# Re-pacing an expert-retrieval kernel: weight splits between VectorE and GpSimd, later one-hots, sums in DRAM

## The chip, the cores and the metric

The kernel runs on one core of a Trainium2 chip. The metric is the device time of one execution in microseconds (us), the median of several runs. The engines of a core run their own instruction queues in order: PE (TensorE, matmuls), DVE (VectorE), ACT (ScalarE), POOL (GpSimd) and SP (SyncE, which here only issues DMAs). POOL issues all indirect DMAs of this kernel, gathers and scatters.

## The reference, cut to what matters

Two layers. Each computes token mixers (attention of two kinds and a retention), an output projection, and then an expert retrieval ("PEER") that holds most of the work and all of the change:

```python
q = (h @ wq).reshape(t, 8, 2, 128)
s = einsum('thpd,hpnd->thpn', q, subkeys)          # two halves of a key, 128 values each
s_top, i_top = top_k(s, 16)                        # per half
cand = s_top[:, :, 0, :, None] + s_top[:, :, 1, None, :]
best, pos = top_k(cand, 16)                        # 16 experts of 128*128 per head, 8 heads
gate = softmax(best)
a = gelu(einsum('cd,chkd->chk', h, u[expert]))     # u, v: (16384, 1024) each
out = einsum('chk,chkd->cd', gate * a, v[expert])
```

Layer 0 has 768 tokens (6 tiles of 128: 0 to 3 latent, 4 and 5 context), layer 1 has 512 (tiles 0 to 3).

## The kernel before, in words

The retrieval is done densely: every 128x128 grid point (i, j) is an expert; for each column j the kernel multiplies 128 rows of u with all tokens of the "dense" tiles (four in layer 0, three in layer 1), takes Gelu, multiplies by a table of gates that is zero where a token did not pick the expert, and multiplies with 128 rows of v. Each layer runs four stages, which this document calls U0, U1 (upass, columns 0 to 63 and 64 to 127 of u) and V0, V1 (vpass, all 128 columns of v, for the first and the second group of tiles; groups are (2,3,4) and (5,0,1) in layer 0, (2,3) and (1,0) in layer 1). All matmuls are fp16 with each operand split into a high and a low half (three products). So every column of u and v is loaded (tile s), its high half made by ACT and its low half `hl` by DVE (L143 in U, L1114 in V); PE waits for both.

The gates come by three ways, spread through the stages as generators that a main loop advances a fixed number of steps per column (`tick`, with the rates `RATES`, `SRATES`, `RRATE`):

- Routing (`routing`, in U0): the query weights wq and the subkeys are split too (`wsplit`: ACT scales and casts, POOL subtracts, L153), PE makes scores (tiles rw, sc), DVE takes the top 16 (`top16`) and `pick` forms expert numbers and gates.
- Tiles 2 and 3: `Onehot.block` multiplies two one-hot matrices on PE, 8 tokens at a time; DVE makes the one-hots (L1194, L1198). There are 32 blocks for each half of the columns; those of half 0 end in a multiplication by DVE (L1213), those of half 1 in a copy by ACT (L1211). All 64 run in U1, one per column.
- The other tiles have a table in DRAM, 128x128x128 numbers. `Table.put` scatters one head's gates with 16 indirect DMAs (L1248, 128 numbers each); the first DMA of a head waits until the 16 of the head before it have landed. A token can pick an expert in several heads, so `pick` adds up equal experts before (128 small operations per tile, tile gjk, L919). V0 and V1 read the tables back. Tiles 4 and 5 (layer 0) and 1 (layer 1) are dense and put gates (table<-gs).
- Tiles 0 and 1 (layer 0) and 0 (layer 1) are "picked": `gather` fetches each of a token's 128 rows of u by an indirect DMA (L946, 128 rows of 4 KB into one of three buffers r), DVE multiplies it with h and sums (L952, two steps behind the gather), and the results are put (table<-a). h is held in PSUM (tile hp), so this operation has one SBUF input.

There are 384 gathers and 768 puts, all in POOL's one queue, in an order that the tile framework fixes when the kernel is built. DVE's queue is in order too: an L952 whose row has not landed holds up the `hl` behind it, and PE waits for that.

`queue_behind` orders a gather or put behind the last low-half split that was noted in `lo_ins`, in the planner's time only, with no semaphore.

Of the kernel before, what the change touches and what calls it, by code (L numbers as in the profile page):

```python
# [23 lines left out]
WS = 64.0  # L24
# [14 lines left out]
WLAG = 2  # L39
WADA = 7  # L40
# [6 lines left out]
class Hybrid:  # L47
# [89 lines left out]
    def split(self, hi, lo, src, scale=1.0, lo_eng=None):  # L137
        nc = self.nc
        nc.scalar.activation(hi, src, AF.Copy, scale=scale)  # L139
        if scale == 1.0:  # L140
            (lo_eng or nc.vector).tensor_tensor(lo, src, hi, op=OP.subtract)  # L141
        else:
            nc.vector.scalar_tensor_tensor(lo, src, scale, hi, op0=OP.mult, op1=OP.subtract)  # L143


    def wsplit(self, hi, lo, w, scale=WS, dve=False):
# [6 lines left out]
        self.lo_ins = nc.gpsimd.tensor_tensor(lo, w, hi, op=OP.subtract)  # L153
# [83 lines left out]
    def layer(self, l, last):  # L237
        with ExitStack() as es:
# [17 lines left out]
            self.vp = self.pool(es, "vs", 2)  # L256
            self.sp = self.pool(es, "sc", 2)
# [433 lines left out]
    def wout(self, l, es, last):  # L691
# [6 lines left out]
        def first(t):  # L698
# [13 lines left out]
            for c in (0, 512):  # L712
# [4 lines left out]
                v = pool.tile([128, 512], F32, name="wov")  # L717
# [41 lines left out]
    def routing(self, l, pool, ps, tiles, rp):  # L759
# [7 lines left out]
        def queries(b):  # L767
            sk = pool.tile([128, 128], F32, name="sk", bufs=3)
# [3 lines left out]
            self.wsplit(skh, skl, sk, SKS)  # L772
            ws = []
            for k in (0, 4):
                w = pool.tile([128, 4, 128], F32, name="wq", bufs=4)
# [3 lines left out]
                self.wsplit(wh, wl, w)  # L779
# [66 lines left out]
    def pick(self, l, t, sv, si, pool):  # L846
# [62 lines left out]
        if t in self.picked:  # L909
            ix = self.lp.tile([128, 16, 8], I32, name="ix", bufs=2)  # L910
# [58 lines left out]
    def peer(self, es, l, last, h2s):  # L969
        nc = self.nc  # L970
        self.hpp = self.pool(es, "hp", 1, space=PSUM)
# [8 lines left out]
        with ExitStack() as e:  # L980
# [8 lines left out]
            while self.unscored:  # L989
                self.step(self.rg, 1)  # L990
        h2s.close()
# [9 lines left out]
        with ExitStack() as e:  # L1001
            ps = self.pool(e, "ups", 4, space=PSUM)
            self.upass(l, 1, ps, "pa", PRATE[l], more)
        pws.close()
        self.accp = self.pool(es, "acc", 1, space=PSUM)
        for n, tiles in enumerate(self.groups):
            self.need(tiles)
            if n == 1 and not last:
                r = lambda: self.gp.tile([128, D], F32, name="r")
                vec = [self.srow(r(), 0, self.hpp.tile([128, D], F32, name="hp")), self.srow(r(), 1)]  # L1010
# [13 lines left out]
    def upass(self, l, half, ps, tag, rrate, more=None):  # L1024
# [5 lines left out]
        sb = {1: 4, 2: 2, 3: 2, 4: 1}[nd - first]  # L1030
        steps = iter(self.onehot) if half else iter(())
        def load(jj):
            u = self.vp.tile([128, KC, 128], F32, name="s4", bufs=3)
# [6 lines left out]
        for jj in range(64):  # L1040
# [5 lines left out]
            pa = ps.tile([128, 512], F32, name=tag)  # L1046
            for k in range(KC):
                self.mm3(pa[:, :nd * 128], uh[:, 0, k], uh[:, 1, k], hh[:, k], hl[:, k], k == 0, k == KC - 1)
# [10 lines left out]
            if jj >= 1:  # L1059
# [6 lines left out]
    def weights(self, tiles, j):  # L1066
# [3 lines left out]
        b = self.lp.tile([128, 2, n, 2, 128], F32, name="h2U" + "hl"[j // 2 % 2])  # L1070
        g, u = b[:, 0], b[:, 1].rearrange("p s j t -> p (s j t)").rearrange("p (j s t) -> p j s t", j=2, t=128)
# [7 lines left out]
        return g, u.rearrange("p j s t -> p s j t"), a  # L1079
# [20 lines left out]
    def vpass(self, l, tiles, n):  # L1100
# [4 lines left out]
        def load(j):  # L1105
            if j % 2 == 0:
                self.pr = self.weigh(tiles, j, *gs.pop(0))
# [229 lines left out]
```

## Time and profile before

| | |
|---|---|
| median of 3 runs | 5107.54 us (5106.78 to 5112.42) |
| profiled execution | 5100.45 us, of which the span of instructions is 5098.7 us |
| busy over the span | PE 82%, DVE 65%, ACT 38%, POOL 35% |
| granted TensorE clock, mean | 0.91 of full speed |

The profile is of one execution, and its own time is the one that a sum over its rows has to be made against. PE's 82% is a mean over stages. The stages of the retrieval, read from the first and the last matmul of each, begin as follows (us from the span's start): layer 0 U0 614, U1 1271, V0 1812, V1 2455 to 2980; layer 1 U0 3434, U1 3921, V0 4386, V1 4735 to 5085. What lies between is projection and attention.

### The profile page before, as it was taken

To read this page: it belongs to the slowest core of one execution; us is meant where nothing else is said; L and a number is where in the kernel's file an instruction comes from. 1 tells how busy PE (TensorE), PEld (TensorE's weight loads), DVE (VectorE), ACT (ScalarE), POOL (GpSimd) and SP (SyncE) were. 2 spreads that over 40 slices of the span, in tenths; PEclk is the share of its full clock that TensorE was granted. 3 is DMA by queue.
4 is the path that set the end of the run, shared out by engine and by line. 5 is a ranking of instruction groups with operands and counts; after the bars stand their busy time and mean duration, and the time that the engine had idled before them with its cause. 6 is when DMAs were issued, how large, how long until landed. Compare 5 with 4: busy or idle time off the path is not lost. (4 is left out here: it accounts for less than half of the span.)

```text
span 5098.7 us, 74857 instructions
## 1 busy us (share of the span) xinstructions
PE 4160.3 (82%) x27326; PEld 2297.0 (45%) x27326; DVE 3334.4 (65%) x7769; ACT 1935.6 (38%) x3191; POOL 1776.3 (35%) x1680
## 2 busy tenths in 40 slices
PE   4987898981687777799899989878866587899898
PEld 3664554740343333344344456646543354444343
DVE  6677559691786666655565544654976587667565
ACT  4556343420122222233333346644432123455444
POOL 3224133477456676620000012333257645400000
PEclk9996899995898889899999999879988798999999
DMA  7831443321477788897788842134543477668787
GB/s 254 298 102 34 150 131 98 116 76 31 153 250 247 250 281 262 272 324 239 241 265 257 252 134 81 43 113 138 172 144 116 143 238 254 226 218 254 254 274 237
DMA packets 512322, 971.54 MB, mean 191 GB/s; under 512 B 73824, under 2 KB 295488, under 8 KB 511952
## 3 DMA queue, kind: packets, MB, share of 16 engines
q1 hardware_dynamic: 422464, 759.66, 46.2%
q0 software_dynamic: 80032, 201.86, 12.4%
q10 hardware_dynamic: 9456, 5.24, 0.4%
q8 instruction: 214, 3.51, 0.3%
q14 instruction: 156, 1.28, 0.1%
HBM read 861.77 MB, written 104.78 MB: 190 GB/s over the span
## 5 line engine op out<-in xcount | busy, mean ns | idle before, releaser
L1126 PE MATMUL acc<-hl,gst 128*128 128x512 f16 x7680 | 1710.7, 385 | 152.5 <-DVE hl L1114 105.8
L1126 PEld LDWEIGHTS <-gst 128*128 128x128 f16 x7680 | 760.6, 99 | 1101.9 <-issue 217.9
L952 DVE SCALAR_TENSOR_TENSOR r<-r,hp 128x1024 f32<-128x1024 f32 x384 | 466.2, 1218 | 580.0 <-DMA r<-peer_u,ix 579.4
L1113 ACT ACTIVATE hl<-s 128x1024 f16<-128x1024 f32 x512 | 538.0, 1051 | 698.5 <-PE acc L1126 392.2
L1114 DVE TENSOR_TENSOR hl<-s,hl 128x1024 f16<-128x1024 f32 x512 | 626.3, 1224 | 244.8 <-ACT hl L1113 243.4
L946 POOL DMA_INDIRECT r<-peer_u,ix x384 | 421.9, 1099 | 488.9 <-DVE r L952 339.5
L168 PE MATMUL pa<-h2Uh,hl 128*128 128x512 f16 (+1 forms) x1024 | 384.2, 376 | 192.9 <-DVE hl L143 192.8
L160 POOL TENSOR_TENSOR rstd<-rstd,mhalf 128x1 f32<-128x1 f32 x26 | 14.2, 546 | 1352.1 <-DVE rstd L159 1348.2
L1248 POOL DMA_INDIRECT table<-a,to x384 | 428.9, 1117 | 149.7 <-issue 110.7
L1248 POOL DMA_INDIRECT table<-gs,to x384 | 410.4, 1069 | 188.1 <-issue 108.8
L168 PE MATMUL pw<-h2Uh,hl 128*128 128x512 f16 (+1 forms) x1024 | 376.4, 368 | 67.1 <-DVE hl L143 67.0
L143 DVE SCALAR_TENSOR_TENSOR hl<-s,hl 128x1024 f16<-128x1024 f32 x256 | 313.7, 1226 | 172.0 <-ACT hl L139 172.0
L168 PEld LDWEIGHTS <-hl 128*128 128x128 f16 x2048 | 209.9, 102 | 477.9 <-DVE hl L143 272.3
L166 PE MATMUL pa<-h2Uh,hl 128*128 128x512 f16 (+1 forms) x1024 | 387.8, 379 | 8.7 <-ACT hl L139 8.7
L166 PE MATMUL pw<-h2Uh,hl 128*128 128x512 f16 (+1 forms) x1024 | 376.9, 368 | 14.0 <-ACT gst L1054 13.7
L167 PE MATMUL pa<-h2Ul,hl 128*128 128x512 f16 (+1 forms) x1024 | 385.7, 377 | 0.0
L167 PE MATMUL pw<-h2Ul,hl 128*128 128x512 f16 (+1 forms) x1024 | 375.7, 367 | 0.0
L153 POOL TENSOR_TENSOR wl<-wst,wh 128x512 f16<-128x512 f32 x96 | 127.9, 1344 | 504.4 <-ACT wh L152 468.5
L167 PEld LDWEIGHTS <-hl 128*128 128x128 f16 x2048 | 210.8, 103 | 205.2 <-issue 52.8
L166 PEld LDWEIGHTS <-hl 128*128 128x128 f16 x2048 | 210.8, 103 | 204.5 <-issue 39.1
L168 PE MATMUL pj<-wh,hTl 128*128 128x256 f16 x1072 | 295.7, 276 | 1.9 <-DVE hTl L141 1.6
L166 PE MATMUL pj<-wh,hTh 128*128 128x256 f16 x1072 | 295.8, 276 | 1.3 <-ACT hTh L139 1.3
(298 smaller groups left out, 7596.0 us busy)
## 6 DMA issues: line engine op xcount, KB each, us to landing
s<-peer_v SPq DMA_DIRECT2D x512, 512.0 KB, 4.7
s<-ut SPq DMA_DIRECT2D x256, 512.0 KB, 4.1
table<-zero SPq DMA_DIRECT2D x48, 1024.0 KB, 8.2
wq<-peer_wq SPq DMA_DIRECT2D x128, 256.0 KB, 3.6
spill<-gst SPq DMA_DIRECT2D x112, 256.0 KB, 4.3
wst<-w_in SPq DMA_DIRECT2D x96, 256.0 KB, 3.1
h2Ul<-table SPq DMA_DIRECT2D x192, 128.0 KB, 3.4
h2Uh<-table SPq DMA_DIRECT2D x192, 128.0 KB, 3.5
```

The lines of the kernel that those rows point to most:

```text
L143: nc.vector.scalar_tensor_tensor(lo, src, scale, hi, op0=OP.mult, op1=OP.subtract)
L153: self.lo_ins = nc.gpsimd.tensor_tensor(lo, w, hi, op=OP.subtract)
L160: nc.gpsimd.tensor_tensor(r, r, self.mhalf[:, :w], op=OP.pow)
L166: nc.tensor.matmul(out, ah, bh, start=start, stop=False)
L167: nc.tensor.matmul(out, ah, bl, start=False, stop=False)
L168: nc.tensor.matmul(out, al, bh, start=False, stop=stop)
L946: self.queue_behind(nc.gpsimd.indirect_dma_start(out=r, out_offset=None, in_=self.i["peer_u"], in_offset=bass.IndirectOffsetOnAxis(ap=ix[: ...
L952: nc.vector.scalar_tensor_tensor(r, r, 1.0, hp, op0=OP.mult, op1=OP.mult, accum_out=a[:, d // 16, d % 16:d % 16 + 1])
L1113: nc.scalar.activation(vh[:, 0], v, AF.Copy)
L1114: nc.vector.tensor_tensor(vh[:, 1], v, vh[:, 0], op=OP.subtract)
L1126: nc.tensor.matmul(acc[s][hf], pr[:, w, s, j % 2], vh[:, x, hf * 512:hf * 512 + 512], start=j == 0 and i == 0, stop=j == 127 and i == 2)
L1248: ins = o.nc.gpsimd.indirect_dma_start(out=self.d, out_offset=bass.IndirectOffsetOnAxis(ap=to[:, k, h:h + 1], axis=0), in_=values[:, c + s ...
```

## The change

- **Weight splits change engines.** The low halves of wq and the subkeys go from POOL to DVE. The low halves of the first 24 columns of u in each U0 go from DVE to POOL (ACT scales and casts in two operations instead of one).
- **One-hots of half 1 come later.** U1 runs only the 32 blocks of half 0, one every second column; the 32 of half 1 run in V0's columns 0 to 61, one every second column. They get PSUM of their own (`ohp`), and U1's matmuls have 2 PSUM buffers where they had 4.
- **Repeated experts of dense tiles are added up in DRAM.** Tiles 4, 5 and 1 (layer 1) skip the 128 operations; heads 1 to 7 are put with an accumulating DMA (`compute_op` add), head 0 with a plain one. Picked tiles keep the 128 operations.
- **The gather's h moves from PSUM to SBUF** (tile hg); its result tile `a` has one buffer instead of two. Buffers of wq, subkeys, one-hots and wov are fewer.
- **The rates change**, and splits of u and v are noted in `lo_ins`, so that gathers and puts are ordered along all of U and V.

```diff
-RATES = {0: (1.0, 1.4, 1.4, 1.4, 0.0, 0.0), 1: (1.0, 1.0, 0.8, 0.8, 0.0, 0.0)}
-SRATES = {0: (2.5, 2.6, 1.7, 2.2, 4.0, 4.0), 1: (2.5, 2.5, 1.4, 1.6, 4.0, 4.0)}
-RRATE = (1.2, 1.0)
+RATES = {0: (0.8, 1.0, 1.5, 1.5, 0.0, 0.0), 1: (0.6, 1.2, 0.4, 0.8, 0.0, 0.0)}
+SRATES = {0: (2.0, 2.9, 1.6, 1.8, 4.0, 4.0), 1: (1.5, 1.8, 0.9, 1.2, 4.0, 4.0)}
+RRATE = (1.3, 1.05)
+UPOOL = 24
...
-    def wsplit(self, hi, lo, w, scale=WS, dve=False):
+    def wsplit(self, hi, lo, w, scale=WS, dve=False, lo_eng=None):
...
-        self.lo_ins = nc.gpsimd.tensor_tensor(lo, w, hi, op=OP.subtract)
+        return (lo_eng or nc.gpsimd).tensor_tensor(lo, w, hi, op=OP.subtract)
...
-            self.wsplit(skh, skl, sk, SKS)
+            self.wsplit(skh, skl, sk, SKS, lo_eng=nc.vector)
...
-                w = pool.tile([128, 4, 128], F32, name="wq", bufs=4)
+                w = pool.tile([128, 4, 128], F32, name="wq", bufs=2)
...
-                self.wsplit(wh, wl, w)
+                self.wsplit(wh, wl, w, lo_eng=nc.vector)
...
-                self.sq += [self.tables[t].put(h, self.rt[t][2], self.rt[t][0], h, 8) for h in range(8)]
+                self.sq += [self.tables[t].put(h, self.rt[t][2], self.rt[t][0], h, 8, OP.add if h else OP.bypass) for h in range(8)]
...
+        if t not in self.picked:
+            nc.vector.tensor_copy(gs, sg)
+            self.rt[t] = gs.rearrange("p k h -> p (k h)"), ix, to
+            return
...
-        h = self.gp.tile([128, D], F32, name="r")
+        h = self.lp.tile([128, D], F32, name="hg", bufs=1)
         nc.scalar.dma_start(h, self.h2d[t])
-        hp = self.hpp.tile([128, D], F32, name="hp")
-        nc.scalar.activation(hp, h, AF.Copy)
-        a = self.lp.tile([128, 8, 16], F32, name="a", bufs=2)
+        a = self.lp.tile([128, 8, 16], F32, name="a", bufs=1)
...
-                nc.vector.scalar_tensor_tensor(r, r, 1.0, hp, op0=OP.mult, op1=OP.mult,
+                nc.vector.scalar_tensor_tensor(r, r, 1.0, h, op0=OP.mult, op1=OP.mult,
...
-        steps = iter(self.onehot) if half else iter(())
+        steps = self.onehot.blocks(0) if half else iter(())
...
-            self.split(uh[:, 0], uh[:, 1], u, US)
+            if not half and jj < UPOOL:
+                self.lo_ins = self.wsplit(uh[:, 0], uh[:, 1], u, US)
+            else:
+                self.lo_ins = self.split(uh[:, 0], uh[:, 1], u, US)
...
-            if jj >= 1:
+            if jj % 2:
                 next(steps, None)
...
-            nc.vector.tensor_tensor(vh[:, 1], v, vh[:, 0], op=OP.subtract)
+            self.lo_ins = nc.vector.tensor_tensor(vh[:, 1], v, vh[:, 0], op=OP.subtract)
...
+        steps = self.onehot.blocks(1) if n == 0 else iter(())
...
-                in_=values[:, c + step * k:c + step * k + 1], in_offset=None)
+                in_=values[:, c + step * k:c + step * k + 1], in_offset=None, compute_op=how)
```

What stands where, in the order in which each engine's instructions are built. First POOL in layer 0, where the puts of the dense tiles meet the first gathers; before:

```order
L1248 DMA table_4_102<-gs,to 2097152x1 x16
L1248 DMA table_5_103<-gs,to 2097152x1 x80
L946 DMA r<-peer_u,ix 128x1024 x3
L1248 DMA table_5_103<-gs,to 2097152x1 x32
L946 DMA r<-peer_u,ix 128x1024 x17
L1248 DMA table_0_100<-a,to 2097152x1 x3
```

The same place of the changed kernel (L1270 is its put, L950 its gather):

```order
L1270 DMA table_4_102<-gs,to 2097152x1 x48
L950 DMA r<-peer_u,ix 128x1024
L1270 DMA table_4_102<-gs,to 2097152x1 x2
L950 DMA r<-peer_u,ix 128x1024
L1270 DMA table_4_102<-gs,to 2097152x1 x2
```

The first gather moved from behind 224 puts to behind 58, and from there on a gather stands between every two or three puts. On DVE the first L952 stood at the split of the last column of U0; its counterpart (L956) now stands 15 columns earlier.

Second, POOL in layer 0 in the middle of V0, where tile 0's gathers end; of the changed kernel:

```order
L950 DMA r<-peer_u,ix 128x1024
L1270 DMA table_0_100<-a,to 2097152x1 x42
L287 MEMSET zero 128x512
L1270 DMA table_0_100<-a,to 2097152x1 x5
L950 DMA r<-peer_u,ix 128x1024 x17
L1270 DMA table_1_101<-a,to 2097152x1
L950 DMA r<-peer_u,ix 128x1024
```

Before, gathers and puts of tile 0 ran on into those of tile 1 with no such block. Now 47 puts of table 0 stand together, and behind them 17 gathers of tile 1 with no put between.

Third, DVE in layer 0 in V0's second half (about column 75); before:

```order
L1114 TENSOR_TENSOR hl<-s_21390,hl 128x1024
L1088 TENSOR_TENSOR h2Ul<-P,h2Ul 128x512
L1091 TENSOR_TENSOR h2Ul<-h2Ul 128x256
L141 TENSOR_TENSOR gst<-h2Uh,gst 128x768
L1114 TENSOR_TENSOR hl<-s_21429,hl 128x1024
L1114 TENSOR_TENSOR hl<-s_21457,hl 128x1024
```

and in the changed kernel (L1132 is hl, L1100 and L1103 are the table products, L956 the gather's product):

```order
L1132 TENSOR_TENSOR hl<-s_21491,hl 128x1024
L956 SCALAR_TENSOR_TENSOR r,a<-r,hg 128x1024
L1100 TENSOR_TENSOR h2Ul<-P,h2Ul 128x512
L956 SCALAR_TENSOR_TENSOR r,a<-r,hg 128x1024
L1103 TENSOR_TENSOR h2Ul<-h2Ul 128x256
L1132 TENSOR_TENSOR hl<-s_21527,hl 128x1024
L956 SCALAR_TENSOR_TENSOR r,a<-r,hg 128x1024
L142 TENSOR_TENSOR gst<-h2Ul,gst 128x768
```

Before, no gather was left in V0's second half; now all 128 products of tile 1 stand there, between columns 65 and 121.

## Rows read from the trace of the kernel before

**Rows 1.** The profile page: span, and busy time, share and instructions of each engine.

```profile
span 5098.7 us, 74857 instructions
PE 4160.3 (82%) x27326; PEld 2297.0 (45%) x27326; DVE 3334.4 (65%) x7769; ACT 1935.6 (38%) x3191; POOL 1776.3 (35%) x1680
```

**Rows 2.** Stretches: length, busy (count) PE, PEld, DVE, ACT, POOL; clock, DMA, GB/s.

```profile
614.00:1166.00 552.00, 500.20 (x4138) 299.59 (x4136) 423.30 (x2207) 211.68 (x417) 256.46 (x242) 0.95 0.35 105
1166.00:1271.00 105.00, 0.00 (x0) 0.00 (x0) 2.46 (x5) 1.62 (x2) 74.07 (x78) 0.51 0.07 17
1271.00:1812.00 541.00, 410.39 (x2556) 190.14 (x2557) 399.56 (x855) 120.06 (x202) 316.07 (x289) 0.88 0.70 226
1812.00:2455.00 643.00, 538.94 (x2303) 233.46 (x2303) 394.25 (x567) 196.02 (x249) 291.51 (x258) 0.93 0.82 274
3434.00:3921.00 487.00, 372.96 (x3246) 251.11 (x3244) 354.84 (x1574) 194.11 (x414) 215.54 (x203) 0.91 0.48 148
3921.00:4386.00 465.00, 319.49 (x2583) 194.43 (x2584) 308.69 (x498) 113.65 (x203) 270.15 (x254) 0.84 0.64 205
4386.00:4735.00 349.00, 335.00 (x1539) 151.04 (x1539) 231.55 (x247) 169.70 (x197) 22.18 (x19) 0.98 0.72 229
```

**Rows 3.** DVE's waits, stretch 1157 to 1280: us in total, times, longest.

```profile
DVE r L952 <- DMA r<-peer_u,ix: 105.1, 1, 105.1
```

**Rows 4.** PE's and DVE's waits: PE 3434 to 3921, then DVE 3434 to 4386.

```profile
PE pw L168 <- DVE hl L143: 39.8, 4, 31.3
DVE r L952 <- DMA r<-peer_u,ix: 207.0, 46, 45.3
```

**Rows 5.** Timeline of POOL, 1177 to 1180: start, us, instruction, idle time before it.

```profile
1177.71 0.96 POOL L1248 DMA_INDIRECT table<-gs,to  x1 [2.17 <-issue]
1178.97 0.96 POOL L1248 DMA_INDIRECT table<-gs,to  x1 [0.30 <-issue]
```

**Rows 6.** Timeline of POOL, 2058 to 2075.

```profile
2058.14 0.95 POOL L1248 DMA_INDIRECT table<-a,to  x1 [0.30 <-issue]
2059.40 1.57 POOL L946 DMA_INDIRECT r<-peer_u,ix  x1 [0.30 <-issue]
...
2073.22 0.98 POOL L946 DMA_INDIRECT r<-peer_u,ix  x1 [0.30 <-issue]
```

**Rows 7.** Timeline of DVE, 2057 to 2080.

```profile
2057.75 1.22 DVE L952 SCALAR_TENSOR_TENSOR r<-r,hp 128x1024 f32<-128x1024 f32 x1 [3.30 <-DMA r<-peer_u,ix]
...
2058.90 1.22 DVE L1114 TENSOR_TENSOR hl<-s,hl 128x1024 f16<-128x1024 f32 x1
...
2078.66 1.22 DVE L952 SCALAR_TENSOR_TENSOR r<-r,hp 128x1024 f32<-128x1024 f32 x1 [5.11 <-DMA r<-peer_u,ix]
```

**Rows 8.** Groups by line, shapes apart: count, busy us, mean ns, idle before.

```profile
L143 DVE SCALAR_TENSOR_TENSOR hl<-s,hl 128x1024 f16<-128x1024 f32 x256 | 313.7, 1226 | 172.0 <-ACT hl L139 172.0
L153 POOL TENSOR_TENSOR wql<-wq,wqh 128x512 f16<-128x512 f32 x128 | 160.7, 1274 | 323.1 <-ACT wqh L152 222.8 <-PE rw L168 93.2 <-PE rw L167 5.4
L1194 DVE TENSOR_TENSOR oi<-iox,sT 128x1024 f16<-128x1024 f16 x128 | 88.3, 690 | 0.0
L1198 DVE TENSOR_TENSOR og<-oj,gT 128x1024 f16<-128x1024 f16 x128 | 88.1, 688 | 0.0
L1194 DVE TENSOR_TENSOR oj<-iox,sT 128x512 f16<-128x512 f16 x128 | 54.1, 423 | 0.0
L1213 DVE TENSOR_TENSOR P<-pw,P 128x512 f32<-128x512 f32 x64 | 44.1, 689 | 5.2 <-PE pw L1205 5.2
L141 DVE TENSOR_TENSOR gst<-P,gst 128x512 f16<-128x512 f32 x64 | 44.1, 689 | 24.1 <-ACT gst L139 24.1
```

**Rows 9.** Instructions on the tile gjk alone, stretch 614 to 1166 (DVE busy).

```profile
614.00:1166.00 552.00, 109.48 (x768) 0.95 0.35 105
```

**Rows 10.** POOL's groups by line, stretch 1812 to 2200.

```profile
L1248 POOL DMA_INDIRECT table<-a,to x118 | 134.3, 1138 | 40.0 <-issue 34.8 <-DMA table<-a,to 2.5 <-DVE a L957 2.4
L946 POOL DMA_INDIRECT r<-peer_u,ix x117 | 129.7, 1109 | 75.4 <-DVE r L952 47.4 <-issue 20.4 <-DVE hl L1114 2.6
```

More of the change, by code (lines that the diff above doesn't have):

```diff
@@ L256, in layer @@
             self.vp = self.pool(es, "vs", 2)
+            self.nv = 3
             self.sp = self.pool(es, "sc", 2)
@@ L716, in first @@
                     self.mm3(p, yT[0][:, k], yT[1][:, k], wh, wl, k == 0, k == KC - 1)
-                v = pool.tile([128, 512], F32, name="wov")
+                v = pool.tile([128, 512], F32, name="wov", bufs=1)
                 nc.vector.tensor_tensor(v, p, self.mod2[:, c:c + 512], op=OP.mult)
@@ L767, in queries @@
         def queries(b):
-            sk = pool.tile([128, 128], F32, name="sk", bufs=3)
+            sk = pool.tile([128, 128], F32, name="sk", bufs=2)
             nc.sync.dma_start(sk, self.i["skT"][l][b])
@@ L909, in pick @@
         if t in self.picked:
-            ix = self.lp.tile([128, 16, 8], I32, name="ix", bufs=2)
+            ix = self.lp.tile([128, 16, 8], I32, name="ix", bufs=len(self.picked))
             nc.vector.tensor_scalar(ix, ef, float(l * 16384), None, op0=OP.add)
@@ L990, in peer @@
                 self.step(self.rg, 1)
+        pws.close()
+        self.pw = self.pool(es, "ohp", 2, space=PSUM)
         h2s.close()
@@ L1001, in peer @@
         with ExitStack() as e:
-            ps = self.pool(e, "ups", 4, space=PSUM)
+            ps = self.pool(e, "ups", 2, space=PSUM)
             self.upass(l, 1, ps, "pa", PRATE[l], more)
-        pws.close()
         self.accp = self.pool(es, "acc", 1, space=PSUM)
@@ L1009, in peer @@
                 r = lambda: self.gp.tile([128, D], F32, name="r")
-                vec = [self.srow(r(), 0, self.hpp.tile([128, D], F32, name="hp")), self.srow(r(), 1)]
+                vec = [self.srow(r(), x) for x in range(2)]
                 self.rg.append(self.ada(1, range(6), vec, r, lambda: self.sp.tile([128, D], F16, name="gst", bufs=GST)))
@@ L1045, in upass @@
             uh = uhs.pop(0)
-            pa = ps.tile([128, 512], F32, name=tag)
+            pa = ps.tile([128, nd * 128], F32, name=tag)
             for k in range(KC):
-                self.mm3(pa[:, :nd * 128], uh[:, 0, k], uh[:, 1, k], hh[:, k], hl[:, k], k == 0, k == KC - 1)
+                for i, (x, h) in enumerate(((0, hh), (0, hl), (1, hh))):
+                    for c in range(0, nd * 128, 512):
+                        d = min(c + 512, nd * 128)
+                        nc.tensor.matmul(pa[:, c:d], uh[:, x, k], h[:, k, c:d], start=k == 0 and i == 0,
+                                         stop=k == KC - 1 and i == 2)
             if not half:
@@ L1069, in weights @@
         n = len(tiles)
-        b = self.lp.tile([128, 2, n, 2, 128], F32, name="h2U" + "hl"[j // 2 % 2])
-        g, u = b[:, 0], b[:, 1].rearrange("p s j t -> p (s j t)").rearrange("p (j s t) -> p j s t", j=2, t=128)
+        b = self.lp.tile([128, KC * 64 * len(self.dense)], F32, name="h2U" + "hl"[j // 2 % 2])
+        g = b[:, 0:n * 256].rearrange("p (s j t) -> p s j t", j=2, t=128)
+        u = b[:, n * 256:n * 512].rearrange("p (j s t) -> p j s t", j=2, t=128)
         for s, t in enumerate(tiles):
@@ L1106, in load @@
             if j % 2 == 0:
-                self.pr = self.weigh(tiles, j, *gs.pop(0))
+                *w, self.spare = gs.pop(0)
+                self.pr = self.weigh(tiles, j, *w)
+                if j == 62:
+                    self.drain(steps)
                 if j + 2 < 128:
                     gs.append(self.weights(tiles, j + 2))
-            v = self.vp.tile([128, D], F32, name="s4", bufs=3)
+            if j % 2 and self.spare is not None:
+                v = self.spare
+            else:
+                v = self.vp.tile([128, D], F32, name="s4", bufs=self.nv)
             vh = self.vp.tile([128, 2, D], F16, name="hl", bufs=3)
@@ L1127, in vpass @@
                                          start=j == 0 and i == 0, stop=j == 127 and i == 2)
+            if j % 2:
+                next(steps, None)
             self.tick(self.rg, 0.4)
@@ L1138, in vpass @@
         for s, t in enumerate(tiles):
-            x = self.vp.tile([128, D], F32, name="s4", bufs=3)
+            x = self.vp.tile([128, D], F32, name="s4", bufs=self.nv)
             self.load_x(x, t)
-            v = self.vp.tile([128, D], F32, name="s4", bufs=3)
+            v = self.vp.tile([128, D], F32, name="s4", bufs=self.nv)
             for hf in range(2):
@@ L1177, in prep, with blocks @@
         self.sT[t] = sT, gT
-    def __iter__(self):
-        for half in range(2):
-            for s in range(2):
-                for tb in range(0, 128, TB):
-                    self.block(half, s, tb)
-                    yield
+    def blocks(self, half):
+        for s, t in enumerate(self.tiles):
+            while t not in self.sT:
+                self.o.step(self.o.rg, 1)
+            for tb in range(0, 128, TB):
+                self.block(half, s, tb)
+                yield
     def block(self, half, s, tb):
@@ L1241, in clear, with put @@
             yield
-    def put(self, h, to, values, c, step):
+    def put(self, h, to, values, c, step, how=OP.bypass):
         o = self.o
```

15 lines of the change are left out of this document (7 added, 8 removed).

## Prediction

> **What bounds the kernel now.** I read the page's totals first. PE is busy 82% of 5098.7 us, POOL 35% [rows 1]: no engine is the bound over the whole span, so I read stage by stage in the table of stretches [rows 2]. In layer 0 PE works 500 of 552 us in U0, nothing in the 105 us after it, 410 of 541 in U1 and 539 of 643 in V0; in layer 1, 373 of 487 in U0, 319 of 465 in U1 and 335 of 349 in V0. Only the last is PE's own. DVE's busy time never fills a stage either, so I went to the waits. The gap of 105 us is one wait: the first product of a gather (L952) stands in DVE's queue, its row has not landed, and everything behind it on DVE, the next `hl` too, stands still [rows 3]. The row is late because its gather is behind 224 puts on POOL, which in those 105 us did 78 DMAs [rows 2]. In layer 1 the same product costs DVE 207 us over U0 and U1 [rows 4]. So the kernel is set, outside V0 and V1's PE work, by how fast POOL walks through gathers and puts and by where they stand in its queue.
>
> **The price of a DMA on POOL.** A put takes 0.96 us and 0.30 us pass before the next; at a change of head 2.17 us pass instead, 1.87 more, since the puts of the head before must land [rows 5]. In V0, with DVE's work beside it, puts cost 1.14 and gathers 1.11 [rows 10]. I take 1.11 + 0.30 = 1.41 us for a DMA that waits for nothing. One gather's loop (issue at 2073.22, product at 2078.66) takes 5.4 us [rows 6, 7]; with three buffers of r a gather cannot come more often than every (5.4 + 1.2)/3 = 2.2 us.
>
> **h in SBUF.** A put beside L952, whose second operand is in PSUM, took 0.95 us; the gather behind it, beside `hl`, which reads two SBUF operands, 1.57 [rows 6, 7]. The changed product reads two SBUF operands like `hl` and takes as long (1.22 against 1.22). So I charge POOL for every product that runs while POOL works: 0.45 us, less than the 0.6 of this pair because a product does not always meet a whole DMA. Bounds: 0, if the row of L952 speaks for all products, and the full 1.22.
> The Trainium skill (page "SBUF — State Buffer", section "Who interferes with whom") says that a DVE instruction with two SBUF inputs contends with a GpSimd instruction that reads SBUF, and one with a single SBUF input does not; the two rows agree in kind. It also describes a lock in which the later one waits for the whole instruction: by that alone a product would cost 1.22, not 0.45.
>
> **Part by part.** Counts of DMAs per stage are counted in the order of the changed kernel, between the places where the stages' matmuls begin.
>
> Layer 0 U0. DVE loses 128 additions of equal experts, 109.48/384 = 0.285 us each [rows 9], 36 us (before, three tiles' additions ran here; now two picked tiles'), and 24 `hl` of 1.23 [rows 8], 29 us. It gains 64 splits of wq (a 128x512 operation, 0.69) and 32 quarter-size ones of the subkeys, 52 us, and 16 products, 20 us. DVE's 423 us of 552 hardly change (+7). POOL loses 64 times 1.27 us and gains 24 splits of a 128x1024 tile, by doubling 1.27 some 2.5 us each, 60 us. But the additions of the two picked tiles now bunch in columns 40 to 56, counted in the order: 16 of them a column are 4.6 us, with an `hl` and a product 7.1, while PE needs 24 matmuls of 0.218 (below), 5.2. Bounds: -52 (all of PE's idle time goes) and +32 (16 columns by 2, the bunch on the path). I take -10, as the three buffers of `hl` cover a little of the bunch and the columns before it lose their additions.
>
> The gap. The first gather is behind 58 puts, not 224, and its product 15 columns before the end of U0: 58 times 1.41 is 82 us, and those puts start while U0 runs. The wait of 105 us goes: -105. What is late next is the gather stream itself, which now runs along U1.
>
> Layer 0 U1. Now 63 gathers and 187 puts stand in it. 250 times 1.41 is 352 us; 12 changes of head by 1.87, 22; an accumulating write's landing may be later, which no row shows: between nothing and the 5.4 us of a gather's whole loop; taken as another 1.87 per head (nearest to the landing of the plain put), 22; 63 products by 0.45, 28. Sum 424, against 541: -117. PE would need less: a 512-column matmul is 335.00/1539 = 0.218 us [rows 2], 64 columns with 24 of them 334 us; 64 one-hot blocks cost the rest of 410, 76 us, so 32 cost 38: 372. So POOL sets this stage, and the one-hots taken out are worth nothing here; two PSUM buffers instead of four for PE likewise, as long as PE waits for POOL's products through DVE.
>
> Layer 0 V0. The 32 one-hot blocks are in it, and the products of tile 1, that were spread over U1 and V0, stand in its last third. Columns 0 to 34: 48 gathers at 3.5 us (in V0 before, 388 us went to 117 gathers with 118 puts [rows 10], 3.3 each) and 0.45 each for the port, 190 us. Columns 34 to 65 hold 47 puts and no product: PE's, 31 by (502/128 = 3.9 and half a block, 0.6), 140 us. Columns 65 to 121: 125 gathers and 97 puts, 222 times 1.41 = 313; six heads by 3.7, 22; the port 58; a wait for the product as before, 47.4/117 each [rows 10], 51: together 444. The order lets some run ahead during columns 34 to 65, so 430. The last 7 columns 27. Sum 787, against 643: +144. Bounds of the last third: 128 times the loop's 2.2 to 2.4 us (307) and, with the full port, 128 times 0.77 more (530).
>
> Layer 1 U0. The products stand in columns where rows have landed; the wait of 39.8 us of PE for an `hl` held by one goes [rows 4]: -40. Bounds 0 and the whole idle time of 114. The 24 `hl` and the splits of wq change places as above, +23 on DVE, which is busy 355 of 487 us and covers it.
>
> Layer 1 U1. 75 gathers and 113 puts: 188 times 1.36 (POOL's mean is 270.15/254 = 1.06 here [rows 2], and 0.30) is 256; seven heads by 1.87 twice, 26; port 34. Sum 316; with the first product's wait 320, against 465: -145. PE needs 319 less half its one-hots, 281.
>
> Layer 1 V0 was PE's; it gets 32 blocks, 35 us at its higher clock, and 32 gathers that lie under them: +35. V1 of both layers, projections and attention stay.
>
> Sum: -10 - 105 - 117 + 144 - 40 - 145 + 35 = -238. The profiled execution took 5100.45; 4862 after. It lies 7 us under the median of the runs (5107.54), so the median is to be about 4870.
>
> **The rivals.**
> *The products contend with nothing that POOL needs.* For it: the row of 0.95 beside L952. Against it: 1.57 beside `hl` with the same kind of operands. Then 0.45 falls away for the products in POOL-bound stretches, 63 + 48 + 128 + 75 = 314: -141, 4730.
> *The last third of V0 goes by the loop.* Few puts stand between the gathers there, so that the three buffers set the pace: 320 instead of 430, 4760.
> *The splits given to DVE bind U0.* They stand in the chain wq, score, top 16, so nothing need cover them. For it: in U0 DVE is the busiest after PE. Then layer 0's U0 takes 55 more than before (52 + 32 - 29), not 10 less, and layer 1's 25 more instead of 40 less: +130, 5000.
> *An accumulating write is dear on POOL.* All but the first head of a dense tile are such puts, and no row shows one. 281 of them lie in the two POOL-bound U1 (175 and 106). My -238 is used up at 238/281 = 0.85 us more for each. If one costs twice the 0.96 of a plain put, as a read and a write of each number might, it is +270: 5140, slower. Against it: POOL's time is that of describing 128 numbers, which is the same for both.
> *The port locks for the whole product*, 314 by (1.22 - 0.45): +242, 5111, no change. The section of the Trainium skill named above is what speaks for this. Against it the 1.57: it paid 0.61 for a neighbour of 1.22.
> *The change does not do what it says:* the gap of 105 returns behind the 58 puts: 4975.
>
> **How the numbers follow.** The forecast 0.42; free port 0.17; loop-bound third 0.13; U0 bound by DVE 0.13; dear accumulation 0.08; full lock 0.05; gap returns 0.02. Of these, the time of the likeliest is 4870; from 4715 (the free port with its spread) to 5010 (U0 bound by DVE) lie 0.85 before their own spread, about 0.8 with it. What a measurement can tell from no change is about 0.2%, 10 us, by the spread of the three runs. Slower by more: dear accumulation and a part of the lock, 0.10; same 0.03; faster 0.87.
>
> **What would show it.** Right: no wait of DVE of over 20 us at the end of U0; U1 of layer 0 near 424 us with POOL working nearly without pause; V0 of layer 0 near 790, longest in its last third; U1 of layer 1 near 320; DMAs beside L956 near 1.4 to 1.6 us; the time between heads 2.2 to 4. Wrong: accumulating puts over 1.5 us each; a head change of over 6; PE waiting for DVE's `wql` in U0; a V0 that stays at 640, or V1 held by table 1's last puts.

## The result and the profile after

The changed kernel took 4979.75 us (median of 4 runs, 4971.35 to 4986.18), the kernel before on the same chip 5107.16 us; the ratio is 0.9749, 95% interval 0.9731 to 0.9766. The forecast was 4870: the sign and the range held, the gain was 127 us instead of about 238. The profiled execution took 4971.35 us.

The page's totals of the changed kernel, in the form of [rows 1], and its stretches, each from the first matmul of a stage to that of the next or to its own last one, in the form of [rows 2] (U0, U1, V0, V1 of layer 0; U0, U1, V0 of layer 1):

```profile
span 4969.6 us, 74031 instructions
PE 4163.8 (84%) x27326; PEld 2290.3 (46%) x27326; DVE 3290.9 (66%) x7148; ACT 1981.0 (40%) x3236; POOL 2045.1 (41%) x1536
```

```profile
612.00:1191.00 579.00, 499.34 (x4135) 301.43 (x4134) 453.49 (x2084) 229.81 (x438) 214.45 (x129) 0.93 0.44 114
1191.00:1675.00 484.00, 383.96 (x2049) 175.03 (x2046) 226.50 (x331) 100.98 (x137) 382.89 (x259) 0.92 0.71 179
1675.00:2433.00 758.00, 588.13 (x2815) 252.11 (x2816) 508.77 (x776) 213.11 (x311) 493.54 (x392) 0.89 0.80 270
2433.00:2966.00 533.00, 501.14 (x2305) 225.41 (x2303) 319.06 (x400) 187.31 (x195) 17.34 (x17) 0.97 0.77 246
3427.00:3878.00 451.00, 373.12 (x3268) 252.78 (x3267) 339.93 (x1386) 212.79 (x434) 159.01 (x98) 0.94 0.52 146
3878.00:4237.00 359.00, 292.16 (x2053) 172.19 (x2052) 234.76 (x350) 96.43 (x137) 284.73 (x195) 0.92 0.83 242
4237.00:4587.00 350.00, 349.29 (x2048) 165.45 (x2047) 293.54 (x381) 184.35 (x255) 160.40 (x114) 0.99 0.79 260
```

PE's busy time is the same to 4 us; what moved is its idle time. The gap is gone: U1 follows U0 at once. The table puts the change against the forecast, stage by stage, in us (a stage runs here to the first matmul of the next one, so that V0 of layer 0 has the start of V1 in it, 666 us before; lengths from the start times of the matmuls):

| stage | before | after | change | forecast |
|---|---|---|---|---|
| layer 0 U0 and gap | 657 | 579 | -78 | -115 |
| layer 0 U1 | 541 | 484 | -57 | -117 |
| layer 0 V0 | 666 | 789 | +123 | +144 |
| layer 1 U0 | 487 | 451 | -36 | -40 |
| layer 1 U1 | 465 | 359 | -106 | -145 |
| layer 1 V0 | 348 | 365 | +17 | +35 |
| all else | | | +8 | 0 |

So three stages gave 37, 60 and 39 us less than forecast, and the two V0 cost 39 less. For layer 0's U1, POOL's groups by line hold most of the reason (in the form of [rows 10]):

```profile
L1270 POOL DMA_INDIRECT table<-gs,to x164 | 273.0, 1665 | 72.1 <-issue 48.7 <-DMA table<-gs,to 22.6 <-DMA r<-peer_u,ix 0.9
L950 POOL DMA_INDIRECT r<-peer_u,ix x68 | 80.1, 1178 | 20.7 <-issue 18.3 <-DVE r L956 0.6 <-DVE hl L144 0.6
L1270 POOL DMA_INDIRECT table<-a,to x27 | 31.1, 1151 | 8.2 <-issue 7.3 <-DMA r<-peer_u,ix 0.6 <-DMA table<-a,to 0.3
```

A put of a dense tile takes 1.67 us, where plain puts of `a` in the same stretch take 1.15. By the order of the puts in the trace, 16 of the 164 are head 0 of table 5 and plain (1.17 us on the mean); the other 148 accumulate and take 1.72. POOL's busy time and the time lost between DMAs are 383 + 101 = 484 us: the whole stage.

### The profile page after: what moved, and what is told of

Read it like the earlier page. It is cut to its first block, busy times and chain, and to the rows that moved or that the text cites. A ratio compares the mean times of both kernels' runs of the same rounds, so it can differ in the third digit from the quotient of the medians.

```text
span 4969.6 us, 74031 instructions
## 1 busy us (share of the span) xinstructions
PE 4163.8 (84%) x27326; PEld 2290.3 (46%) x27326; DVE 3290.9 (66%) x7148; ACT 1981.0 (40%) x3236; POOL 2045.1 (41%) x1536
## 5 line engine op out<-in xcount | busy, mean ns | idle before, releaser
L956 DVE SCALAR_TENSOR_TENSOR r<-r,hg 128x1024 f32<-128x1024 f32 x384 | 469.0, 1224 | 585.9 <-DMA r<-peer_u,ix 581.8
L1131 ACT ACTIVATE hl<-s 128x1024 f16<-128x1024 f32 x512 | 538.5, 1053 | 735.0 <-PE acc L1145 373.6
L1270 POOL DMA_INDIRECT table<-gs,to x384 | 636.3, 1657 | 232.9 <-issue 117.6
L1132 DVE TENSOR_TENSOR hl<-s,hl 128x1024 f16<-128x1024 f32 x512 | 625.8, 1223 | 143.0 <-ACT hl L1131 140.6
L950 POOL DMA_INDIRECT r<-peer_u,ix x384 | 484.0, 1260 | 449.3 <-DVE r L956 155.6
L1058 PE MATMUL pw<-h2Uh,hl 128*128 128x512 f16 (+1 forms) x2048 | 592.4, 366 | 65.3 <-DVE hl L144 57.1
L1058 PE MATMUL pa<-h2Uh,hl 128*128 128x512 f16 (+1 forms) x2048 | 601.6, 372 | 47.3 <-DVE hl L144 45.6
L1270 POOL DMA_INDIRECT table<-a,to x384 | 493.2, 1284 | 176.9 <-issue 129.8
L168 PE MATMUL pj<-wl,hTh 128*128 128x256 f16 x1072 | 295.2, 275 | 0.0
L1065 ACT ACTIVATE gst<-pa 128x512 f32<-128x512 f32 (+1 forms) x128 | 69.4, 542 | 530.4 <-PE pa L1058 437.5
L154 POOL TENSOR_TENSOR hl<-s,hl 128x1024 f16<-128x1024 f32 x48 | 105.2, 2195 | 297.0 <-ACT hl L153 253.6
L140 ACT ACTIVATE hl<-s 128x1024 f16<-128x1024 f32 x208 | 219.0, 1053 | 12.4 <-DMA s<-ut 11.3
```

Of the source, the lines that this page charges most:

```text
L154: return (lo_eng or nc.gpsimd).tensor_tensor(lo, w, hi, op=OP.subtract)
L168: nc.tensor.matmul(out, ah, bl, start=False, stop=False)
L950: self.queue_behind(nc.gpsimd.indirect_dma_start(out=r, out_offset=None, in_=self.i["peer_u"], in_offset=bass.IndirectOffsetOnAxis(ap=ix[: ...
L956: nc.vector.scalar_tensor_tensor(r, r, 1.0, h, op0=OP.mult, op1=OP.mult, accum_out=a[:, d // 16, d % 16:d % 16 + 1])
L1058: nc.tensor.matmul(pa[:, c:d], uh[:, x, k], h[:, k, c:d], start=k == 0 and i == 0, stop=k == KC - 1 and i == 2)
L1131: nc.scalar.activation(vh[:, 0], v, AF.Copy)
```

## The experiments

The kernel before took 5107.16, 5261.2, 5298.0 and 5101.0 us on the four chips that the runs fell on, the changed one 4979.75 and 4992.12 on two of them; so times are compared on one chip, and stages of kernels from different chips with the care that this asks for (the last section shows one thing in which the chips differ). The times are medians of 4 runs of each kernel and 7 of the kernel before (4 on the first chip); the stage lengths, in us, are from the start times of the matmuls of the profiled execution, as above:

| kernel | median us | ratio to before, 95% | L0 U0 | U1 | V0 | L1 U0 | U1 | V0 |
|---|---|---|---|---|---|---|---|---|
| plain writes | 4919.9 | 0.9330 (0.9278-0.9381) | 634 | 406 | 798 | 463 | 326 | 363 |
| additions on DVE | 4972.95 | 0.9443 (0.9407-0.9479) | 613 | 440 | 799 | 473 | 326 | 367 |
| h in PSUM | 4928.56 | 0.9366 (0.9317-0.9415) | 588 | 460 | 774 | 457 | 351 | 363 |
| before with sums in DRAM | 5320.51 | 1.0100 (1.0056-1.0145) | 851 | 581 | 592 | 617 | 397 | 345 |
| changed, second chip | 4992.12 | 0.9439 (0.9400-0.9477) | 579 | 490 | 800 | 462 | 362 | 366 |
| faster puts in U0 | 4890.11 | 0.9257 (0.9218-0.9295) | 600 | 444 | 705 | 485 | 347 | 363 |
| wq's low halves on POOL | 5006.98 | 0.9475 (0.9438-0.9513) | 591 | 489 | 794 | 459 | 357 | 371 |
| u's low halves on DVE | 4960.98 | 0.9380 (0.9342-0.9419) | 574 | 494 | 805 | 449 | 356 | 362 |
| two buffers of a | 4904.45 | 0.9618 (0.9598-0.9638) | 576 | 482 | 722 | 452 | 360 | 365 |
| three edits | 4838.97 | 0.9477 (0.9452-0.9502) | 577 | 444 | 708 | 465 | 348 | 365 |
| three edits, slower picks | 4801.64 | 0.9407 (0.9383-0.9431) | 528 | 453 | 716 | 457 | 350 | 364 |

The first four ran on one chip, the next four on another, the last three on a third, which is the one on which the kernel before takes 5101 us. The same change is worth 2.5% on the first chip and 5.6% on the second, since the kernel before is slower there and the changed one hardly.

**The accumulating write alone.** The changed kernel with plain writes:

```diff
-                in_=values[:, c + step * k:c + step * k + 1], in_offset=None, compute_op=how)
+                in_=values[:, c + step * k:c + step * k + 1], in_offset=None, compute_op=OP.bypass)
```

> The changed kernel with plain writes for every head (the tables then hold, for an expert that a token picked in several heads, only the gate that came last, instead of the sum); the order of the instructions on each engine is the same. Theory, the accumulating write is dear on POOL: a put of a dense tile falls from 1.55 us without a neighbour to 0.96; 163 of them in layer 0's U1 and 74 in layer 1's give 96 and 44 us, less where PE's 384 and 292 us are reached; together -110 to -140, about 4850. Rival, the shared port took the missing gain: nothing changes but the puts, 4965 to 4985.

U1 came out at 406 and 326 us, 84 and 36 below the 490 and 362 of the changed kernel on the second chip. POOL's group of these puts in layer 0's U1 (1247 to 1653):

```profile
L1270 POOL DMA_INDIRECT table<-gs,to x160 | 182.1, 1138 | 80.1 <-issue 53.3 <-DMA table<-gs,to 26.2 <-DMA r<-peer_u,ix 0.6
```

The mean fell from 1665 to 1138 ns with the same instructions in the same order, 0.53 us a put, and 160 of them are 84 us: as much as the whole difference of the stage. Without the 16 puts that are plain in both kernels it is 0.59 us (1.72 against 1.13). The wait for a head to land (22.6 us in the changed kernel, 26.2 here) did not fall with it: nothing shows that an accumulating write lands later. The total did not reach the expected 4850, because U0 of layer 0 took 634 us; between 840 and 915 us PE worked 37 of 75 us there, and its own longest waits in that stretch wait for nothing that the profile shows:

```profile
PE rw L168 <- issue: 16.5, 20, 1.9
PE rw L169 <- issue: 14.3, 15, 1.8
```

That is a loss of another kind than the price of a put; it is taken up in the last section.

**The sums back on DVE.** The changed kernel with the additions of dense tiles and plain writes:

```diff
-        if t not in self.picked:
-            nc.vector.tensor_copy(gs, sg)
-            self.rt[t] = gs.rearrange("p k h -> p (k h)"), ix, to
-            return
...
-                self.sq += [self.tables[t].put(h, self.rt[t][2], self.rt[t][0], h, 8, OP.add if h else OP.bypass) for h in range(8)]
+                self.sq += [self.tables[t].put(h, self.rt[t][2], self.rt[t][0], h, 8) for h in range(8)]
```

> The changed kernel with the repeated experts of dense tiles added up by DVE again (128 operations a tile) and plain writes. Theory, dear writes and a U0 that DVE bounds: the two U1 give back 96 and 44 us, U0 pays 73 us in layer 0 and 36 in layer 1 where DVE has no room: about -30, 4950. Rival, DVE has room in U0: -110 to -140, 4850. Rival, writes cost nothing that counts: +70 to +110, 5070.

U1 gave 50 and 36 us back, the two U0 took 34 and 11 more; 4973 lies between the first and the third theory's numbers and nearest to the first. But most of the 34 us is not DVE's. In U0 of layer 0 (614 to 1227) PE again has waits for nothing that the profile shows, 32 us of them:

```profile
PE rw L169 <- issue: 11.5, 15, 1.2
PE rw L168 <- issue: 10.1, 11, 2.5
PE rw L167 <- issue: 10.0, 13, 1.2
```

So the totals of the two ways of summing are about the same on these chips, but what the additions cost DVE in U0 is not shown, and whether DVE has room there, as the first rival says, stays open.

**That part alone, on the kernel before.** The same lines as in the change, put into the kernel before.

> The kernel before with this one part of the change: dense tiles' repeated experts are added up by accumulating writes. Theory: DVE is relieved of 256 operations of 0.285 us in layer 0's U0 and 128 in layer 1's, but the first gather of layer 0 stands behind 224 puts of which 210 now cost 0.59 more, 124 us; the gap at the end of U0 grows from 105 to between 150 and 200, and the time is 5150 to 5200. Rival, the write is no dearer where it counts: U0 ends earlier, 5040 to 5080.

It is slower, by 59 us or 1.0% (0.6 to 1.5). The expected times, 43 to 93 us above 5107, hold as a difference; the gap grew beyond the expected 200 us. DVE's wait for the first gather, the stretch that it leaves idle, and POOL in it:

```profile
DVE r L956 <- DMA r<-peer_u,ix: 212.1, 2, 211.5
```

```profile
1099.00:1307.00 208.00, 0.94 (x5) 0.40 (x4) 3.61 (x9) 2.44 (x5) 164.09 (x107) 0.51 0.23 8
```

```profile
1100.32 1.55 POOL L1252 DMA_INDIRECT table<-gs,to  x1 [0.30 <-issue]
1102.17 1.55 POOL L1252 DMA_INDIRECT table<-gs,to  x1 [0.30 <-issue]
```

The 105 us of [rows 3] have become 211.5. With almost no work on the other engines, a put is 1.55 us against the 0.96 of [rows 5]: 0.59 more, and the next one follows 0.30 later as before. The stretch holds 104 puts, so 61 of the 106 us are the price of the write; the rest was not taken apart, and the two profiles are from different chips.

**h's place.** The changed kernel with half of h in PSUM:

```diff
-        h = self.lp.tile([128, D], F32, name="hg", bufs=1)
-        nc.scalar.dma_start(h, self.h2d[t])
+        hr = self.gp.tile([128, D], F32, name="r")
+        nc.scalar.dma_start(hr, self.h2d[t])
+        h = self.hpp.tile([128, 512], F32, name="hp")
+        nc.scalar.activation(h, hr[:, :512], AF.Copy)
...
-                nc.vector.scalar_tensor_tensor(r, r, 1.0, h, op0=OP.mult, op1=OP.mult,
+                rv = r.rearrange("p (a b) -> p a b", b=512)
+                nc.vector.scalar_tensor_tensor(rv, rv, 1.0, h[:, None, :].to_broadcast([128, 2, 512]), op0=OP.mult, op1=OP.mult,
```

> The changed kernel with the product's second operand in PSUM, of which there is room for 512 of h's 1024 columns, used twice (so the picked experts' products are of another h), and one PSUM buffer for the one-hots. Theory, POOL's DMAs wait for a product that reads two SBUF operands: gathers and puts of a beside a product fall from a mean of 1.35 to 1.4 us to 1.0, and where POOL bounds (both U1 and the last third of V0), some 270 products by 0.37: -70 to -100, 4890. Rival, that time lies under other waits: within 15 us, 4965 to 4995.

V0 of layer 0 fell from 789 and 800 us (the changed kernel on two other chips) to 774, U1 from 484 and 490 to 460, layer 1's U1 from 359 and 362 to 351. That is 47 to 67 us in the POOL-bound stages, less than the expected 70 to 100. POOL's groups by line in V0 of layer 0, first of the changed kernel (1675 to 2433), then of this one (1662 to 2436, which takes in the start of V1):

```profile
L1270 POOL DMA_INDIRECT table<-a,to x214 | 270.9, 1266 | 93.8 <-issue 74.3 <-DMA table<-a,to 17.1 <-DVE h2Ul L1103 2.4
L950 POOL DMA_INDIRECT r<-peer_u,ix x173 | 217.0, 1254 | 135.5 <-DVE r L956 100.6 <-issue 23.8 <-DVE gst L142 4.6
```

```profile
L1274 POOL DMA_INDIRECT table<-a,to x229 | 255.9, 1118 | 105.9 <-issue 77.5 <-DMA table<-a,to 23.7 <-DVE oj L1220 2.6
L952 POOL DMA_INDIRECT r<-peer_u,ix x173 | 197.8, 1143 | 158.2 <-DVE r L959 110.3 <-issue 29.7 <-DMA r<-peer_u,ix 14.3
```

The DMAs are 0.11 to 0.15 us shorter on the mean over all of them, and the wait for a free row (`r <- DVE`) grew by 10 us. So a part of what the port costs seems to lie under the loop of three buffers; that is argued from this one wait, not tried.

**Where U0's time goes.** Two kernels move the low halves back, one the splits of wq and the subkeys to POOL, one those of u to DVE:

```diff
-            self.wsplit(skh, skl, sk, SKS, lo_eng=nc.vector)
+            self.wsplit(skh, skl, sk, SKS)
...
-                self.wsplit(wh, wl, w, lo_eng=nc.vector)
+                self.wsplit(wh, wl, w)
```

> The changed kernel with the low halves of wq and the subkeys on POOL again; gathers and puts stand behind the same instructions. Theory, U0 of layer 0 is long because the additions of the two picked tiles stand together at its end, where DVE is full: the splits cost nothing on DVE, and U0 stays within -10 and +25: 4965 to 5000. Rival, the splits on DVE lengthen the routing: U0 of layer 0 falls by 30 to 50 us and that of layer 1 by 20 to 30: 4900 to 4930.

```diff
-UPOOL = 24
+UPOOL = 0
```

> The changed kernel with the low halves of all columns of u on DVE (24 of 1.23 us a layer leave POOL, where they take 2.2). Theory, as for the kernel above: DVE has room in the first 24 columns, so U0 stays within 10 us, 4965 to 4995. Rival, DVE is short in the routing as well: 29 us for each layer, 5020 to 5040.

Splits of wq on POOL: U0 of layer 0 591 against 579, of layer 1 459 against 462, 15 us in all. So the rival that DVE's splits lengthen the routing is refuted. The low halves of u on DVE: 31 us less than the changed kernel on the same chip, which neither expectation had. 5 of them are in U0 of layer 0, 13 in U0 of layer 1 and 9 in the stretch between V1 and that U0 (451 against 460); layer 0's U1 and V0 are 9 longer. That part of the change costs about 30 us; what in it does so was not taken apart.

**Faster puts.**

```diff
-SRATES = {0: (2.0, 2.9, 1.6, 1.8, 4.0, 4.0), 1: (1.5, 1.8, 0.9, 1.2, 4.0, 4.0)}
+SRATES = {0: (4.0, 2.9, 1.6, 1.8, 4.0, 4.0), 1: (3.0, 1.8, 0.9, 1.2, 4.0, 4.0)}
```

> The changed kernel with the puts of dense tiles advanced faster in U0 (SRATES of U0 4.0 in layer 0 and 3.0 in layer 1, for 2.0 and 1.5): the first gather then stands behind 116 puts, not 58. Theory, POOL's walk sets U1 and its wait of 103 us at the first gather, for expert numbers that DVE has not made, is idle time that puts could use: 58 puts of 1.86 us leave U1 of layer 0 (-80 to -108, until PE's 384 us bound it), 29 leave that of layer 1 (-30 to -50): about 4860. Rival, the puts delay the low halves of u that POOL makes in U0, and PE: no gain, 4960 to 5000.

102 us less than the changed kernel, but not where it was expected: U1 gave 46 and 15 (not 80 to 108 and 30 to 50), the two U0 took 21 and 23 back, and V0 of layer 0 gave 95. The idle time that the edit fills is one wait on POOL, in U0 of the changed kernel (612 to 1191), which stands in no row of the kernel with faster puts:

```profile
POOL r L950 <- DVE ix L913: 103.2, 1, 103.2
```

**The gain in V0.** Faster puts let table 0 be written out earlier, and tile 1's first product writes the one tile `a` that those puts read. Whether that is what shortened V0 was tried by giving `a` its second buffer back, with the old rates:

```diff
-        a = self.lp.tile([128, 8, 16], F32, name="a", bufs=1)
+        a = self.lp.tile([128, 8, 16], F32, name="a", bufs=2)
```

> The changed kernel with two buffers for the gather's results (tile a), as before; 512 bytes a partition. The first product of tile 1 then stands at V0's column 36 instead of 65, behind 335 puts. Theory, V0's length comes from the wait of tile 1's gathers for table 0's last puts, since the one buffer is read by them: V0 of layer 0 goes from about 795 us to about 710, as in the kernel with faster puts, and the time is 80 to 100 us less than the changed kernel's (0.925 to 0.930 of the kernel before where that had 0.944). Rival, the number of DMAs in V0 sets it wherever they stand: within 20 us of the changed kernel.

V0 of layer 0 fell to 722 us, all other stages stayed within 10 of the changed kernel's. The time, 4904.45, is 75 us less than the changed kernel's 4979.75 on the first chip, a little under the expected 80 to 100. The timeline of POOL in the changed kernel at the place of the second piece of order, where the 47 puts end:

```profile
1968.93 0.95 POOL L1270 DMA_INDIRECT table<-a,to  x1 [0.30 <-issue]
1976.57 1.71 POOL L950 DMA_INDIRECT r<-peer_u,ix  x1 [6.68 <-DVE r L956]
```

The last put of table 0 starts at 1968.93, and POOL's next gather waits for a row that DVE frees with the first product of tile 1, at 1975. With two buffers that product starts at 1856, and V0 is 67 us shorter for 512 bytes a partition.

**Together.** The three edits (faster puts, two buffers of a, u's low halves on DVE), and then with one more:

> The changed kernel with three edits: faster puts in U0 (as tried), two buffers of tile a, and all low halves of u on DVE. Expected: U0 574 to 600, U1 444, V0 700 in layer 0, since faster puts alone already had V0 at 704, and 15 to 30 us from the low halves: 4855 to 4880, or 0.920 to 0.923 of the kernel before. Rival, with more room V0 falls to PE's 590 to 650: 0.91.

```diff
-            self.tick(self.rg, rrate)
+            self.tick(self.rg, rrate if half or self.unscored else 0.8)
             self.tick(self.bg, RATES[l][half])
```

> As the kernel with the three edits, and the picks' generator runs 0.8 steps a column, not 1.3 and 1.05, once the scores of U0 are made: 13 additions a column instead of 21, so DVE needs about 5 us a column and PE 5.2, and the rest of the additions goes on in U1. Theory, the bunch of additions lengthens U0 of layer 0 by 2.5 us for some 20 columns: U0 is 30 to 50 us shorter than in the kernel with the three edits, and up to 20 us come back since the gathers start six columns later: 20 to 40 us less in all. Rival, PE has other waits there: within 15 us.

The ratios that the expectations of the second buffer and of the three edits name were taken over from a chip on which the kernel before is slower, and don't apply. The three edits gave 4839, below the expected 4855 to 4880; V0 stayed at 708. The slower picks saved another 37 us: U0 of layer 0 gave 49, 577 to 528, and 9 and 8 were lost in U1 and V0. The same 160 us of U0 in the changed kernel, in the one with three edits, and in the one with all four:

```profile
970.00:1130.00 160.00, 115.97 (x496) 49.72 (x493) 156.88 (x799) 45.59 (x78) 44.34 (x28) 0.87 0.40 107
```

```profile
970.00:1130.00 160.00, 116.55 (x493) 49.95 (x492) 157.59 (x812) 42.15 (x73) 113.03 (x70) 0.85 0.46 109
```

```profile
970.00:1130.00 160.00, 144.43 (x637) 62.64 (x636) 146.94 (x722) 51.80 (x91) 128.40 (x78) 0.96 0.55 121
```

DVE was full and PE idle for 44 us, with three edits as in the changed kernel; with the additions spread (32 of the 256 now run in U1) PE is idle for 16, and its clock is granted at 0.96 instead of 0.85. This kernel takes 4801.64 us, 0.9407 of the kernel before (0.9383 to 0.9431), against 0.9749 for the change as it was made.

**The kernel before on a chip of the experiments.**

> The kernel before, for its profile on this chip, since it took 5107 us on the first chip and 5261 and 5298 on two others, while the changed kernel took 4980 and 4992. Theory, the difference lies where plain puts stand close together and everything else waits for POOL: U0 of layer 0 and the gap behind it (657 us on the first chip from U0's first matmul to U1's) and U0 of layer 1. Rival, the chip is slower throughout: every stage is longer by 2 to 4%.

Its one run fell on a chip on which the kernel before takes 5101, and its stages are those of the first profile to 7 us (U0, gap and U1 together 1202 us against 1199). So it shows no stage for the two chips with 5261 and 5298, and where those 150 to 190 us lie is open; the last section has a hint.

## Why the prediction was right in kind and its gain nearly twice too large

- **What bounds the kernel** was read rightly: POOL's walk through puts and gathers, and their place in its queue. The gap went, U1 became POOL's alone (383 us busy and 101 between DMAs of 484), and the two edits that won most by themselves, faster puts (102 us) and the second buffer (75 us), change that order or a wait in it.
- **The dear accumulating write** was a rival with a chance of 0.08 and a price of 0.96; the price is 0.59 (1.55 against 0.96), below the 0.85 at which it would have decided the sign. The forecast's step "1.41 us for a DMA that waits for nothing" took it as 0. In its place stand 0.59 for each of 148 puts, 87 us, where layer 0's U1 missed by 60: the 22 us for a later landing did not come, nor some of the port's. In layer 1's U1 the 75 such puts cost 36 to 44 us, and the stage missed by 39. The rival's count was off too: it has 175 and 106 accumulating puts in the two U1, but the puts of `a` there (27 and 43) are plain, and so are the 16 of a head 0. The argument against the rival, that describing 128 numbers is the same work for both, was wrong: POOL's queue moved 37632 packets more for the same bytes, 112 for each of the 336 accumulating puts (last section).
- **U0 of layer 0** was to lose 10 us beyond the gap and is 27 us longer. The bunch of additions was in the text with +32 as the far end; the stage with the additions spread is 49 us shorter, so the bunch by itself is over that end. The value taken between the ends was the wrong one: DVE was full from 970 to 1130, as the step itself had worked out (7.1 us a column against PE's 5.2), and the three buffers of `hl` did not carry that. The rival by which the splits bind U0 came near in the total (5000 for 4980), but for the wrong cause: with them on POOL, U0 is not shorter.
- **h in SBUF** was the right mechanism, taken too dear. By my count over the whole trace, DMAs that start within a product take 1.49 (83 puts of `a`) and 1.43 us (89 gathers), against 1.00 and 0.99 with h in PSUM (78 and 71), so a DMA that meets the port pays about the 0.45. But not every product meets one: over the whole execution the indirect DMAs keep POOL busy 1614 us, and 1506 with h in PSUM, 0.28 for each of the 384 products. As stage time the forecast charged 141 us, and h in PSUM gave back 47 to 67. Neither the free port nor the full price of 1.22 for every product holds.
- **V0 of layer 0** (+123 for +144) was right in what makes it long: from tile 1's first product at 1975 to the end of the stage at 2433 are 458 us, for 430 and 27. Inside that sum luck helped: the waits for a free row are 89 us, not 51, and those for a head to land 6, not 22. That a second buffer would have kept the stage at +56 the prediction didn't see, though it had the block of 47 puts in front of it.
- **Layer 1's U0** (-36 for -40) is right by half its mechanism: PE's wait for an `hl`, 39.8 us in [rows 4], is still 17.8, so 22 us came from there; the rest was not taken apart.
- **The later one-hots** were put down as worth nothing in U1 and 35 us in layer 1's V0, which took 17. That part alone wasn't tried.

The rows behind the points on layer 1's U1 (3878 to 4237, and 3877 to 4202 with plain writes), on V0's last third (1975 to 2433) and on layer 1's U0 (3427 to 3878):

```profile
L1270 POOL DMA_INDIRECT table<-gs,to x75 | 131.3, 1750 | 28.2 <-issue 23.6 <-DMA table<-gs,to 4.3 <-DMA r<-peer_u,ix 0.3
L1270 POOL DMA_INDIRECT table<-gs,to x72 | 91.0, 1265 | 30.9 <-issue 23.1 <-DMA table<-gs,to 7.8
POOL r L950 <- DVE r L956: 88.9, 53, 6.7
POOL table L1270 <- DMA table<-a,to: 5.6, 5, 2.5
PE pw L1058 <- DVE hl L144: 17.8, 3, 12.7
```

So the step that failed is the price of a put in the POOL-bound stages, and beside it the value taken for U0's bunch of additions. That the total came within 110 us owes something to luck: the port, charged too dear, and the landing that did not come hid a part of the accumulating writes.

## What to carry to other kernels

Price the new form of an operation on the engine that is the bound of the stage, even if only its option changed: the accumulating write costs 60% more on the queue that it is issued from, and alone, even with DVE relieved of its additions, it made the kernel 1% slower where it ran. A queue that is the bound in one stage and waits 103 us in the stage before is a schedule to be mended first. When buffers are cut to make room, follow each one's last reader into its queue: one tile of 512 bytes held up 128 products.

## What the runs showed of the hardware

- **The accumulating indirect write** of 128 numbers: 1.55 us on POOL with no neighbour, plain 0.96; the wait of a head for the landing is about the same (10 waits of 2.26 us on the mean in layer 0's U1, 2.17 in [rows 5]). The pages also show more packets in POOL's queue for the same megabytes, here of the changed kernel and of the one with plain writes:

```profile
q0 software_dynamic: 117664, 201.86, 15.0%
q0 software_dynamic: 80032, 201.86, 12.6%
```

- **The port.** Puts that start 0.1 us after a product with two SBUF operands took about a microsecond longer. Two pairs from the changed kernel's V0, POOL and then DVE:

```profile
1725.26 1.94 POOL L1270 DMA_INDIRECT table<-a,to  x1 [0.30 <-issue]
1728.79 1.96 POOL L1270 DMA_INDIRECT table<-a,to  x1 [0.30 <-issue]
```

```profile
1725.13 1.22 DVE L956 SCALAR_TENSOR_TENSOR r<-r,hg 128x1024 f32<-128x1024 f32 x1
1728.69 1.21 DVE L956 SCALAR_TENSOR_TENSOR r<-r,hg 128x1024 f32<-128x1024 f32 x1
```

A put of 0.96 that starts 0.1 us into a product of 1.22 ends 0.85 us behind the product's end. That is what a lock for the whole instruction would make, as the Trainium skill has it (page "SBUF — State Buffer", section "Who interferes with whom"); over all DMAs that start within a product it is 0.44 to 0.49 on the mean, since most of them meet only a part of it. In the kernel with h in PSUM a gather that starts within a product took 0.98:

```profile
1727.93 0.98 POOL L952 DMA_INDIRECT r<-peer_u,ix  x1 [0.66 <-DVE r L959]
```

- **PE without instructions.** In the kernel with plain writes PE had 45 waits for nothing shown, of up to 1.9 us each, in 75 us in which POOL issued 43 DMAs and the DMA engines were busy 14%. The changed kernel shows no such stretch on the first chip. Summed over a whole trace, PE's waits for nothing shown split by chip, not by kernel: none in the six traces of the first chip and of the one with 5101 us (kernel before twice, changed kernel, second buffer, three and four edits), and 30 to 106 us in each of the eight traces of the two chips with 5261 and 5298. The largest sum, 106 us in 137 waits, is that of the kernel before with sums in DRAM, the nearest to the kernel before. In U0 of layer 0 the two kernels with plain writes lose 40 and 32 us by them on one chip, and the kernel with accumulating writes and h in PSUM loses 2.4 us there. The kernel before has plain writes. So these waits are a likely part of those 150 to 190 us; the kernel before itself was not profiled there, and what holds PE up stays open.
